# Quarter 0 scaled as rows before it is turned, and a fixed TensorE order around the first and the last products of the first feed-forward

## The chip, the core and the metric

The kernel runs on one core of a Trainium2 chip. Its engines work side by side, each through its own list of instructions in order: TensorE (PE, matrix products; its weight loads are listed as PEld), VectorE (DVE), ScalarE (ACT), GpSimd (POOL) and SyncE (SP, which here only issues DMAs). An instruction waits for what it reads and for the buffer that it writes; the order in each engine's list is made when the kernel is built. The metric is the device time of one execution in microseconds.

## The reference

One step of an encoder layer: a half-step SwiGLU feed-forward, a mixer of two branches (stick-breaking attention and a gated linear recurrence), a second half-step feed-forward, and a last norm. 1024 prompt frames with 16 meta tokens ahead, and 32 frames of a running stream, go through the same weights: T = 1072 tokens of 1024 channels. What the change touches is the first feed-forward and what it hands on:

```
def rmsnorm(x, g):
    y = xf * lax.rsqrt(jnp.mean(xf * xf, axis=-1, keepdims=True) + EPS)
    return (y * g.astype(jnp.float32)).astype(x.dtype)

def half_ffn(x, g, w_gate, w_up, w_down):
    h = rmsnorm(x, g)
    return x + 0.5 * ((jax.nn.silu(h @ w_gate) * (h @ w_up)) @ w_down)

    xp = concatenate([meta_tokens, x_prompt])        # 16 + 1024 rows
    x = half_ffn(x, ffn1_norm, ffn1_w_gate, ffn1_w_up, ffn1_w_down)
    h = rmsnorm(x, mix_norm)
    qa, ka, va, zf, ih, qh, g, ga, gb = split(h @ w_in)
    f = lb + (1.0 - lb) * sigmoid(zf)
```

## The kernel before

**Numbers.** Each factor of a product is split into a high and a low part (`split` L200, `weights` L167), and a product is three matmuls: high by high, high by low, low by high. `weights` loads a 128 by 1024 block of weights to a tile `raw` (two buffers), ACT copies it to `whi` (L184), DVE subtracts for `wlo` (L185); both have three buffers.

**Tiles.** In the first feed-forward the tokens stand in four quarters of QW = 268, and the 1024 channels in two halves (`kh`) of four 128-blocks. A quarter q is pair b = q // 2, side th = q % 2. `B[kh, th, b]` are the split, normalised activations of one half of one quarter (128 channels, four blocks, 268 tokens). Elsewhere tokens go in three tiles TT of 400, 384 and 288.

**Opening (L374 to L516).** Tokens come as rows: two tiles of 128 tokens for each quarter (`rows`), and `odds`, one tile that holds the last 12 tokens of each quarter at partitions 0, 32, 64, 96. POOL clears `odds` first. All these loads are issued on SP's queue, then the weights. `scales` (L392) makes the norm's factor of each token from rows: ACT squares with a running sum, two DVE steps, a power on POOL, four DVE steps. `spread` (L411) brings the factors of a quarter to all partitions: POOL multiplies the identity by the factors (`diag`, in the home of `ys`, shown as `t_ys`), PE multiplies ones by it, ACT copies the result to `R`. `columns` (L436) turns a quarter: for each of eight channel blocks three PE transposes into one PSUM bank, ACT copies the raw values to `x0` (stored to `x0_dram` for the residual), DVE multiplies by gain and R, and each half is then split into `B`. `first_units(0, columns_ahead)` (L487, L505) makes the first 128 gate and up columns: quarter by quarter 24 gate and 24 up matmuls, and ahead of quarter q the spread and the columns of quarter q + 1 (of 0 and 1 for the first). The order on PE is the planner's: it takes what it believes ready, by the program's order. `first_units(1, ...)` follows, `sums` (L456) makes the combinations of quarters for the later units, which take seven block products for eight (L531).

**End of the first feed-forward (L595 to L640).** `mid_dram` holds the 22 middle blocks. Eleven pairs of down weights are multiplied by them and added to `acc` (L633), for three token tiles and eight channel blocks. In the last pair, `after1` (L606) follows each token tile: it stores `acc`, calls `finish_one`, and `normalise` (L212): ACT makes `xh` (L216) and the squares (L222, L225), DVE makes `xl` (L217) and three of the squares' sums, POOL the other sums (L226). The two sum tiles `tot` have two buffers (`raw2`, shown as `t_raw`). The closure put into `waiting` (L234) is the rest: PE adds over partitions with ones, and `scale_rows` (L242) makes R on ACT (Ln, Exp) and POOL. `finish_one` runs all that wait.

**The first w_in products (L648 to L673).** `project_all` with the units of `zf` 0, 1 and 2 goes over token tiles, then units: 24 matmuls, DVE times R (L669), ACT sigmoid. After each token tile `between` calls `finish_one`.

**Order by hand.** `InOrder` (L88) chains PE's instructions in program order while `on` is true; in the parts above it is off. A `NoSync` dependency (`order`) only ties two instructions' places in the plan. `functions` (L109) loads a set of ACT functions.

Of the kernel before, what the change touches and what calls it, by code (L numbers as in the profile page):

```python
# [79 lines left out]
def tile_encoder_step(ctx, tc, x_prompt, x_sample, cache_k, cache_v, state_hgrn, meta_tokens,  # L80
# [70 lines left out]
    functions("natural_log_exp_and_others")  # L151

# [14 lines left out]
    def weights(parts, own=None):  # L167
        raw = wp.tile([P, D], F32, tag="raw", name="raw", bufs=2)
        n = 0
        for src, k in parts:  # L170
# [13 lines left out]
        A.activation(hi, raw, AF.Copy)  # L184
# [21 lines left out]
    homes = {"junk": ("ms", 1), "diag": ("ys", 1)}  # L206
# [55 lines left out]
    def ffn(pool, tiles, acc, xh, xl, R, w_gate, w_up, w_down, own, final, after, opening, later=None):  # L262
# [35 lines left out]
        def down(cs, mids, last):  # L298
            ws = [weights([(w_down[0][c * P:(c + 1) * P, :], 1)], own) for c in cs]
# [59 lines left out]
    with tc.tile_pool(name="f1", bufs=2) as pool:  # L359
# [8 lines left out]
        def load(dst, p0, t0, n):  # L368
            for src, c, r in sources:
                a, b = max(t0, c), min(t0 + n, c + r)  # L370
                if a < b:
                    nc.sync.dma_start(dst[p0 + a - t0:p0 + b - t0], src[a - c:b - c])
# [4 lines left out]
        rows = []  # L377
        for q in range(4):
# [5 lines left out]
            if q == 0:  # L384
                for x in range(4):
                    load(odds, 32 * x, x * QW + 2 * P, ODD)
# [5 lines left out]
        def scales(tiles):  # L392
# [3 lines left out]
            for j, xt in enumerate(tiles):  # L396
                for h in range(2):
                    junk = temp(pool, "junk")
                    A.activation(junk.bitcast(BF16)[:, :512], xt[:, h * 512:(h + 1) * 512], AF.Square,
                                 accum_out=ss[:, h, j:j + 1])  # L400
# [10 lines left out]
        def spread(q, r1, odd):  # L411
            diag = temp(pool, "diag")
            ps = bank(rotate=True)
            for h in range(2):
                c = slice(h * P, (h + 1) * P)
                G.tensor_scalar(diag[:, c], ident, r1[h], None, op0=ALU.mult)
                PE.matmul(ps[:, c], ones, diag[:, c], start=True, stop=True)
            p, c = slice(32 * q, 32 * q + ODD), slice(2 * P, QW)
            G.tensor_scalar(diag[p, c], ident[p, p], odd[p], None, op0=ALU.mult)
            PE.matmul(ps[:, c], ones[p], diag[p, c], start=True, stop=True)  # L420
            A.activation(R[:, q * QW:(q + 1) * QW], ps[:, :QW], AF.Copy)
# [14 lines left out]
        def columns(q):  # L436
            b, th = divmod(q, 2)
            for kh in range(2):
                x0 = f32s("s")
                v = value(kh, th, b)  # L440
                for k in range(4):
                    ps = bank(rotate=True)
                    ks = slice((4 * kh + k) * P, (4 * kh + k + 1) * P)
                    for h in range(2):
                        PE.transpose(ps[:, h * P:(h + 1) * P], rows[2 * q + h][:, ks], ident)
                    p = slice(32 * q, 32 * q + ODD)
                    PE.transpose(ps[:, 2 * P:QW], odds[p, ks], ident[p, p])
                    A.activation(x0[:, k], ps[:, :QW], AF.Copy)
                    V.scalar_tensor_tensor(v[:, k], ps[:, :QW], gains[:, 0, 4 * kh + k:4 * kh + k + 1],
                                           R[:, q * QW:(q + 1) * QW], op0=ALU.mult, op1=ALU.mult)  # L450
                nc.sync.dma_start(x0_dram[:, 4 * kh:4 * kh + 4, q * QW:(q + 1) * QW], x0)
                split(*B[kh, th, b], v)
# [34 lines left out]
        def first_units(c, before):  # L487
            gw = weights([(ffn1_w_gate[0][:, c * P:(c + 1) * P], KC)])
            uw = weights([(ffn1_w_up[0][:, c * P:(c + 1) * P], KC)])
            g = pool.tile([P, T], F32, tag="g", name="g", bufs=4)  # L490
            for q in range(4):
                before(q)
                b, th = divmod(q, 2)
                pss = []
                for wh, wl in (gw, uw):
# [9 lines left out]
        def columns_ahead(q):  # L505
            if q == 0:
                r = scales(rows[0:2] + [odds])
                found.append(r[2])
                spread(0, r[:2], found[0])
                columns(0)  # L510
# [964 lines left out]
```

## Time and profile before

| | us |
|---|---|
| median of three runs (2545.7 to 2548.61) | 2548.09 |
| the profiled execution | 2547.18 |
| its span, first to last instruction | 2545.4 |
| mean granted TensorE clock | 0.997 |
| PE busy in the first 73 us | 51.94 |
| DVE busy from 774 to 784 us, PE busy there | 10.00, 6.29 |

The span is divided among engines by busy time; times in the views are microseconds from the span's start, durations in us or (means) in ns. A line such as "PE a L100 <- POOL b L416: 5.7, 1, 5.7" says that PE's instruction at line 100, which writes a, waited 5.7 us in all for POOL's line 416, once, at longest 5.7. The chain of waits is followed back from the last instruction; its pieces have start, length, and what ran. In a timeline line the bracket is the engine's idle time before the instruction and what ended it. A window of the windows view lists length, then busy time and count for PE, PEld, DVE, ACT and POOL, then the granted clock, the DMA share and GB/s.

### The profile page before, as it was taken

To read this page: it belongs to the slowest core of one execution; us is meant where nothing else is said; L and a number is where in the kernel's file an instruction comes from. 1 tells how busy PE (TensorE), PEld (TensorE's weight loads), DVE (VectorE), ACT (ScalarE), POOL (GpSimd) and SP (SyncE) were. 2 spreads that over 40 slices of the span, in tenths; PEclk is the share of its full clock that TensorE was granted. 3 is DMA by queue.
4 is the path that set the end of the run, shared out by engine and by line. 5 is a ranking of instruction groups with operands and counts; after the bars stand their busy time and mean duration, and the time that the engine had idled before them with its cause. 6 is when DMAs were issued, how large, how long until landed. Compare 5 with 4: busy or idle time off the path is not lost.

```text
span 2545.4 us, 44180 instructions
## 1 busy us (share of the span) xinstructions
PE 2497.2 (98%) x18396; PEld 2397.6 (94%) x18396; DVE 1418.6 (56%) x2635; ACT 815.5 (32%) x1652; POOL 247.0 (10%) x388
## 2 busy tenths in 40 slices
PE   6999999999999999999999999999999999999998
PEld 5999999999998999998888888999999999999998
DVE  4655555577675467764655665557443444444445
ACT  6433333411124233332544543325211111111113
POOL 1000000000003012221000000214111001000100
PEclk9999999999999999999999999999999999999999
DMA  7122222352222111112111214321111111111112
GB/s 200 58 88 68 85 68 90 109 185 84 87 73 90 42 43 55 47 58 59 43 47 43 68 52 150 119 84 42 51 50 38 46 50 50 37 48 50 49 35 77
DMA packets 219182, 179.38 MB, mean 70 GB/s; under 512 B 37270, under 2 KB 202390, under 8 KB 218982
## 3 DMA queue, kind: packets, MB, share of 16 engines
q1 hardware_dynamic: 218950, 176.56, 22.3%
q8 instruction: 144, 2.36, 0.4%
q14 instruction: 56, 0.46, 0.1%
q0 software_dynamic: 32, 0.00, 0.0%
HBM read 137.78 MB, written 38.75 MB: 69 GB/s over the span
## 4 chain that ended last, share of the span: by engine, by line
PE 92%; DVE 5%; ACT 2%; issue 1%; DMA 1%; POOL 0%; SPq 0%; DVEq 0%; ACTq 0%; POOLq 0%
PE ps_z L100 37%; PE ps_mm L100 33%; PE ps_o L100 11%; PE ps_tr L100 8%; PE ps_tr L103 2%; DVE xl L217 1%; PE ps_z L103 1%; DVE wlo L185 1%; ACT whi L184 0%; PE ps_mm L103 0%; DVE left L993 0%; DVE acc L1381 0%; DMA xt<-in_x_prompt_dram 0%; DMA ga<-gate_dram 0%; DVE sd L875 0%
## 5 line engine op out<-in xcount | busy, mean ns | idle before, releaser
L100 PE MATMUL ps_mm<-xh,whi 128*128 128x384 f32 (+2 forms) x1224 | 405.4, 331 | 0.5 <-DVE raw L1201 0.5
L100 PE MATMUL ps_mm<-xh,wlo 128*128 128x384 f32 (+2 forms) x1224 | 399.1, 326 | 0.0
L100 PE MATMUL ps_mm<-xl,whi 128*128 128x384 f32 (+2 forms) x1224 | 398.2, 325 | 0.0
L184 ACT ACTIVATE whi<-raw 128x1024 fp32r<-128x1024 f32 x152 | 158.1, 1056 | 669.5 <-PE ps_z L100 429.4
L100 PEld LDWEIGHTS ps_mm<-xh,whi 128*128 128x128 f32 x1224 | 230.5, 188 | 9.1 <-issue 5.0
L100 PE MATMUL ps_z<-xh,whi 128*128 128x384 f32 (+2 forms) x720 | 234.9, 326 | 4.0 <-ACT whi L184 2.4
L100 PE MATMUL ps_z<-xh,wlo 128*128 128x384 f32 (+2 forms) x720 | 234.0, 325 | 0.1
L100 PE MATMUL ps_z<-xl,whi 128*128 128x384 f32 (+2 forms) x720 | 234.0, 325 | 0.0
L100 PEld LDWEIGHTS ps_mm<-xl,whi 128*128 128x128 f32 x1224 | 230.5, 188 | 1.2
L100 PEld LDWEIGHTS ps_mm<-xh,wlo 128*128 128x128 f32 x1224 | 230.7, 189 | 0.4
L185 DVE TENSOR_TENSOR wlo<-raw,whi 128x1024 fp32r<-128x1024 f32 x152 | 185.8, 1236 | 46.6 <-ACT whi L184 44.1
L100 PEld LDWEIGHTS ps_z<-xh,whi 128*128 128x128 f32 x720 | 136.1, 189 | 5.0 <-ACT whi L184 2.7
L286 POOL TENSOR_TENSOR g<-g,R 128x384 f32<-128x384 f32 (+1 forms) x66 | 77.7, 1178 | 641.4 <-ACT g L116 641.4
L993 DVE TENSOR_TENSOR_SCAN left<-left,oneb 128x512 f32<-128x512 f32 (+6 forms) x112 | 107.3, 958 | 54.8 <-ACT left L116 54.2
L100 PEld LDWEIGHTS ps_z<-xh,wlo 128*128 128x128 f32 x720 | 136.5, 190 | 0.9 <-DVE wlo L185 0.9
L100 PEld LDWEIGHTS ps_z<-xl,whi 128*128 128x128 f32 x720 | 136.2, 189 | 0.2
L287 DVE TENSOR_TENSOR g<-ps_z,g 128x384 f32<-128x384 f32 (+1 forms) x66 | 34.6, 524 | 179.1 <-PE ps_z L100 177.9
L116 ACT ACTIVATE g<-g 128x268 f32<-128x268 f32 (+2 forms) x126 | 58.1, 461 | 192.5 <-DVE g L284 148.3
L100 PE MATMUL ps_z<-ml,whi 128*128 128x384 f32 (+1 forms) x360 | 116.4, 323 | 0.0
L100 PE MATMUL ps_z<-mh,wlo 128*128 128x384 f32 (+1 forms) x360 | 115.8, 322 | 0.0
L100 PE MATMUL ps_z<-mh,whi 128*128 128x384 f32 (+1 forms) x360 | 115.7, 321 | 0.0
L100 PE MATMUL ps_z<-xe,whi 128*128 128x268 f32 (+3 forms) x424 | 111.9, 310 | 0.0
(581 smaller groups left out, 6240.7 us busy)
## 6 DMA issues: line engine op xcount, KB each, us to landing
raw<-in_ffn_w_gate_dram SPq DMA_DIRECT2D x44, 512.0 KB, 3.7
raw<-in_ffn_w_up_dram SPq DMA_DIRECT2D x44, 512.0 KB, 3.6
raw<-in_ffn_w_down_dram SPq DMA_DIRECT2D x44, 512.0 KB, 4.3
raw<-in_w_in_dram SPq DMA_DIRECT2D x44, 512.0 KB, 3.8
mid_dram<-g SPq DMA_DIRECT2D x22, 536.0 KB, 2.7
mid<-mid_dram SPq DMA_DIRECT2D x22, 536.0 KB, 3.7
gate_dram<-gst SPq DMA_DIRECT2D x32, 192.0 KB, 1.9
acc<-x_dram SPq DMA_DIRECT2D x3, 1536.0 KB, 6.7
```

The lines of the kernel that those rows point to most:

```text
L100: return self.queue(nc.tensor.matmul(*args, **more))
L103: return self.queue(nc.tensor.transpose(*args, **more))
L116: i = A.activation(out, in_, func, **more).ins
L184: A.activation(hi, raw, AF.Copy)
L185: V.tensor_tensor(lo, raw, hi.bitcast(F32), op=ALU.subtract)
L217: V.scalar_tensor_tensor(xl[:, k, s], srcs[k], g, xh[:, k, s].bitcast(F32), op0=ALU.mult, op1=ALU.subtract)
L286: G.tensor_tensor(g[:, :n], g[:, :n], R[:, s], op=ALU.mult)
L287: V.tensor_tensor(g[:, :n], pu[:, :n], g[:, :n], op=ALU.mult)
L993: V.tensor_tensor_scan(rev(st[:rows]), rev(st[:rows]), one, 1.0 if carry is None else carry[:rows], op0=ALU.mult, op1=ALU.mult)
```

## The change

It has these parts.

1. The odd rows are loaded on ACT's queue; the first gate and up weights are issued on SP's queue right after quarter 0's rows, ahead of the rows of quarters 1 to 3.
2. Quarter 0: `raw_columns` transposes it unscaled and DVE copies it to `x0`. Then its rows are scaled in place by the norm's factors (ACT one tile, DVE the other and the odd rows), transposed again (`scaled_columns`), and split straight from PSUM: ACT makes high and plain values, DVE the low part. Spread 0 goes.
3. DVE makes the diagonals in place of POOL, in a tile of their own; the Squares of quarters 1 to 3 are tied on ACT behind a given instruction (`behind`).
4. In unit 0, spread and columns of quarter q + 1 stand between the half products of quarter q, and PE's order is fixed from the raw transposes to unit 0's last product. Unit 1's weights are tied behind a late ACT instruction.
5. In the last down pair PE's order is fixed until the zf products are through. The first zf weights are asked for before that pair. The sums over partitions go singly: tile 0's after six blocks of tile 2, the others each after a zf product. The sigmoids wait for the last sum.
6. A first load of an ACT function set goes; two small DVE steps (`lmax`, `causalb`) are tied behind the latest product.

```diff
-    functions("natural_log_exp_and_others")
-    homes = {"junk": ("ms", 1), "diag": ("ys", 1)}
+    homes = {"junk": ("ms", 1)}
...
-    def weights(parts, own=None):
+    def weights(parts, raw=None, own=None, behind=None):
...
+        made = A.activation(hi, raw, AF.Copy).ins
+        if behind is not None:
+            tc.add_manual_dep(made, behind.name, order, reason="order")
...
-                    load(odds, 32 * x, x * QW + 2 * P, ODD)
+                    load(odds, 32 * x, x * QW + 2 * P, ODD, nc.scalar)
+                for raw, w in zip(first, (ffn1_w_gate, ffn1_w_up)):
+                    nc.sync.dma_start(raw.rearrange("p (k m) -> p k m", k=KC),
+                                      w[0][:, :P].rearrange("(k p) m -> p k m", p=P))
...
+        latest = [None]
+        def scales(tiles, behind=None):
...
+                    latest[0] = A.activation(junk.bitcast(BF16)[:, :512], xt[:, h * 512:(h + 1) * 512],
+                                              AF.Square, accum_out=ss[:, h, j:j + 1]).ins
+                    if behind is not None:
+                        tc.add_manual_dep(latest[0], behind.name, order, reason="order")
...
+        def diagonals(q, r1, odd):
+            diag = pool.tile([P, QW], F32, tag="diag", name="diag", bufs=3)
+            for h in range(2):
+                c = slice(h * P, (h + 1) * P)
+                V.tensor_scalar(diag[:, c], ident, r1[h], None, op0=ALU.mult)
...
+        def raw_columns():
+            for kh in range(2):
+                x0 = f32s("s")
+                for k in range(4):
+                    V.tensor_copy(x0[:, k], turned(0, 4 * kh + k))
+                nc.sync.dma_start(x0_dram[:, 4 * kh:4 * kh + 4, :QW], x0)
+
+        def scale_rows_of(r):
+            for kh in range(2):
+                ks = slice(kh * 512, (kh + 1) * 512)
+                latest[0] = A.activation(rows[0][:, ks], rows[0][:, ks], AF.Copy, scale=r[0]).ins
+                V.tensor_scalar(rows[1][:, ks], rows[1][:, ks], r[1], None, op0=ALU.mult)
+                V.tensor_scalar(odds[:ODD, ks], odds[:ODD, ks], r[2][:ODD], None, op0=ALU.mult)
+
+        def scaled_columns():
+            for kh in range(2):
+                h, l = B[kh, 0, 0]
+                v = value(kh, 0, 0)
+                for k in range(4):
+                    g = gains[:, 0, 4 * kh + k:4 * kh + k + 1]
+                    ps = turned(0, 4 * kh + k)
+                    latest[0] = A.activation(h[:, k], ps, AF.Copy, scale=g).ins
+                    V.scalar_tensor_tensor(l[:, k], ps, g, h[:, k].bitcast(F32), op0=ALU.mult, op1=ALU.subtract)
+                    A.activation(v[:, k], ps, AF.Copy, scale=g)
...
                     for kh in range(2):
                         ks = slice(kh * 512, (kh + 1) * 512)
                         product(ps, (wh[:, ks], wl[:, ks]), B[kh, th, b], kh == 0)
+                        between(q, 2 * j + kh)
...
+        def next_columns(q, step):
             if q < 3:
+                if step == 0:
+                    spread(q + 1, diags.pop(0))
+                    if q < 2:
+                        diags.append(scaled_diagonals(q + 2))
+                elif step < 3:
+                    columns(q + 1, step - 1)
+
+        def scaled_diagonals(q):
+            return diagonals(q, scales(rows[2 * q:2 * q + 2], latest[0]), odd_scale)
+
+        PE.on = True
+        raw_columns()
+        r = scales([rows[0], odds, rows[1]])
+        ws = [weights([], first[0], behind=latest[0])]
+        odd_scale = r[1]
+        scale_rows_of([r[0], r[2], r[1]])
+        ws.append(weights([], first[1], behind=latest[0]))
+        scaled_columns()
+        diags = [scaled_diagonals(1)]
+        first_units(0, next_columns, ws)
+        PE.on, PE.last, third = False, None, latest[0]
...
-            finish_one()
             normalise(pool, chunks(acc, t0, n), xh1, xl1, 1, R1, t0, n)
...
             if final:
                 functions("natural_log_exp_and_others")
+                zf_first = weights([(w_in[0][:, COL_ZF:COL_ZF + P], KC)])
+                PE.on = True
...
                 for m in range(KC):
                     one(m, t0, n)
+                    if final and j == 2 and m == 5:
+                        waiting.pop(0)()
...
-                if between:
-                    between()
+                    if between:
+                        between()
...
+                raw_gates.append(z)
+                if not waiting:
+                    if table["name"] != "sigmoid_and_others":
+                        functions("sigmoid_and_others")
+                    while raw_gates:
+                        z = raw_gates.pop(0)
+                        act(z, z, AF.Sigmoid)
...
-        project_all([zf_unit(h) for h in range(3)], TT, True, finish_one)
+        project_all([zf_unit(h) for h in range(3)], TT, True, lambda: waiting and waiting.pop(0)(), [zf_first])
+        PE.on, PE.last = False, None
```

More of the change, by code (lines that the diff above doesn't have):

```diff
@@ L165, in tile_encoder_step @@
     big = Wide
-    def weights(parts, own=None):
-        raw = wp.tile([P, D], F32, tag="raw", name="raw", bufs=2)
-        n = 0
-        for src, k in parts:
+    def weights(parts, raw=None, own=None, behind=None):
+        n, loaded = 0, raw is not None
+        if not loaded:
+            raw = wp.tile([P, D], F32, tag="raw", name="raw", bufs=2)
+        for src, k in () if loaded else parts:
             m = src.shape[-1]
@@ L377, in tile_encoder_step @@
         rows = []
+        first = [wp.tile([P, D], F32, tag="raw", name="raw", bufs=2) for _ in range(2)]
         for q in range(4):
@@ L434, in value, with turned @@
             return last[b] if (kh, th) == (1, 0) else plain[b][:, {(0, 0): 0, (0, 1): 1, (1, 1): 2}[kh, th]]
-        def columns(q):
-            b, th = divmod(q, 2)
+        def turned(q, k):
+            ps = bank(rotate=True)
+            ks = slice(k * P, (k + 1) * P)
+            for h in range(2):
+                PE.transpose(ps[:, h * P:(h + 1) * P], rows[2 * q + h][:, ks], ident)
+            p = slice(32 * q, 32 * q + ODD)
+            PE.transpose(ps[:, 2 * P:QW], odds[p, ks], ident[p, p])
+            return ps[:, :QW]
@@ L503, in first_units @@
             nc.sync.dma_start(mid_dram[c], g)
[L505 to L510, printed above, removed]
-            if q < 3:
-                spread(q + 1, scales(rows[2 * q + 2:2 * q + 4]), found[0])
-                columns(q + 1)
-        found = []
-        first_units(0, columns_ahead)
+        def next_columns(q, step):
+            if q < 3:
+                if step == 0:
[17 more added lines that the diff above has]
+        PE.on, PE.last, third = False, None, latest[0]
         t4s = [sums(b) for b in range(2)]
-        first_units(1, lambda q: None)
+        first_units(1, lambda q, step: None, [weights([(w[0][:, P:2 * P], KC)], behind=third)
+                                              for w in (ffn1_w_gate, ffn1_w_up)])
         constants()
@@ L646, in project, with project_all @@
             project_all([(col, evac)], tiles)
-        def project_all(units, tiles=TT, rotate=False, between=None):
-            ws = [weights([(w_in[0][:, col:col + P], KC)]) for col, _ in units]
+        def project_all(units, tiles=TT, rotate=False, between=None, ws=None):
+            ws = ws or []
+            ws = ws + [weights([(w_in[0][:, col:col + P], KC)]) for col, _ in units[len(ws):]]
             pending = []
```

57 lines of the change are left out of this document (24 added, 33 removed).

## The prediction

> **What bounds the kernel now.** First the busy times of the page: TensorE (PE) is busy 98% of the span, so time can be won only where PE stands still or runs slowly.
>
> ```profile
> PE 2497.2 (98%) x18396; PEld 2397.6 (94%) x18396; DVE 1418.6 (56%) x2635; ACT 815.5 (32%) x1652; POOL 247.0 (10%) x388
> ```
>
> That leaves 2545.4 - 2497.2 = 48.2 us of idle PE. Second, the waits of PE, in the stretches that the diff touches: 0 to 75 us, then 745 to 835 us (total, times, longest).
>
> ```profile
> PE ps_z L103 <- DMA xt<-in_x_prompt_dram: 8.6, 2, 7.0
> PE ps_mm L100 <- POOL t_ys L416: 5.7, 1, 5.7
> PE ps_z L100 <- POOL t_ys L416: 3.8, 1, 3.8
> PE ps_mm L100 <- DVE acc0s L449: 2.8, 1, 2.8
> ```
>
> ```profile
> PE ps_z L100 <- ACT whi L184: 2.4, 1, 2.4
> PE ps_z L100 <- POOL t_raw L226: 1.8, 1, 1.8
> PE ps_z L100 <- DVE t_raw L226: 1.4, 1, 1.4
> ```
>
> Some 21 us of waits stand before the first product and 5.6 around the last products of the first feed-forward. Third, the chain of waits in order of time (start, us) gives the marks to measure against.
>
> ```profile
> 18.06 1.92 PE ps_mm L100 x6
> 19.98 0.84 PE ps_mm L103 x3
> ...
> 37.02 4.97 PE ps_mm L100 x24
> 41.99 2.96 PE ps_z L100 x24
> 44.95 0.76 PE ps_tr L100 x6
> 45.71 0.53 PE ps_z L103 x3
> ...
> 787.58 6.21 PE ps_z L100 x22
> 793.79 8.58 PE ps_mm L100 x48
> ```
>
> Read: 24 products take 4.97 us at first and 2.96 later; a spread (six matmuls of ones by a diagonal) 1.92, later 0.76; a group of three transposes 0.84, later 0.53. **Mark one** is 44.95: quarter 0's gate and up products done, quarter 1's spread and columns done too. **Mark two** is 793.79: the first two zf units have done their first token tile and all three sums of squares are through PE. Fourth, the timeline, for the pace of PE.
>
> ```profile
> 40.54 0.43 PE L100 MATMUL ps_mm<-xh0s,whi 128*128 128x268 f32 x1
> 40.76 0.37 PE L100 MATMUL ps_mm<-xl0s,whi 128*128 128x268 f32 x1
> ```
>
> At 40.5 us PE still runs at half pace: products start 0.22 us apart, later 2.96/24 = 0.12. The spread at 18.06 and the eight groups of transposes behind it, some 7 us, did not end that; 3.8 us of unbroken products from 37.02 did (the matmul at 40.76 is the first shorter one).
>
> **The opening, part by part.** Removed: spread 0, its copy to R and the splits of quarter 0. Added: a second pass of transposes, because quarter 0 is now turned raw (for x0), scaled in place, and turned again; all of it, and everything up to unit 0's last product, in one fixed PE order.
>
> ```profile
> 6.96 0.63 ACT L399 ACTIVATE t_ms<-xt 128x512 bf16<-128x512 f32 x1 [3.65 <-DMA xt<-in_x_prompt_dram]
> 10.09 0.69 PE L103 MATMUL ps_z<-cst,xt 128*128 128x128 f32 x2 [1.58 <-DMA xt<-in_x_prompt_dram]
> 11.56 0.39 PE L103 MATMUL ps_z<-cst,odds 12*128 12x12 f32 x2
> 15.08 0.16 DVE L402 TENSOR_TENSOR ss<-ss 128x3 f32<-128x3 f32 x1 [11.66 <-ACT t_ms L399]
> 17.13 0.16 DVE L408 TENSOR_TENSOR ss<-ss 128x3 f32<-128x3 f32 x1
> 28.23 0.63 ACT L399 ACTIVATE t_ms<-xt 128x512 bf16<-128x512 f32 x1
> 28.77 0.19 ACT L399 ACTIVATION_READ_ACCUMULATOR t_ms<-xt 128x1 f32 x1
> L448 ACT ACTIVATE s<-ps_z 128x268 f32<-128x268 f32 x16 | 6.4, 405 | 1.3 <-PE ps_z L103 0.6
> L947 DVE TENSOR_SCALAR xs<-xs 128x384 f32<-128x384 f32 x8 | 2.8, 354 | 4.7 <-POOL xs L946 4.7
> ```
>
> 1. Each group now needs both row tiles and the odd rows at once. The second row tile is there at 10.09, the odd rows by 11.56 (their landing isn't shown). Their four DMAs go to ACT's queue behind POOL's memset; ACT has nothing before 6.96. The first two weights move ahead of the later rows on SP's queue; they and the odd rows may hold up the second row tile. I take 10.5; bounds 9.7 and 12.5.
> 2. Eight raw groups at 0.83 (0.84 in the chain): to 17.1. DVE copies them out, under PE's pace.
> 3. Six Squares of about 0.75 (0.63 and the accumulator's read) on ACT end near 13; the scale chain takes 17.3 - 15.1 = 2.2, with DVE copies in between about 3; DVE may run a weight split (1.2) ahead of it. Then the rows are scaled, 0.63 a half on ACT, about 0.4 a half twice on DVE (nearest row: 354 ns for 384 columns). The second pass starts near 17.9: 0.8 lost (bounds 0 and 3).
> 4. Eight scaled groups: to 24.5. ACT makes two copies a group, 0.41 each, just under PE's pace. So the first product starts at 24.5, not 37.02.
> 5. Twelve products of 0.22 (gate, first half): to 27.2. Then the fixed order demands spread 1. Its Squares are tied on ACT behind quarter 0's last scaled copy (24.9; the last plain copy 25.2): four of 0.75 to 28.2, chain 2.2 to 30.4, first diagonal on DVE and its hand-over 0.4 (bounds 0.16, the three-column step, and 0.7, two of the 354 ns) to 30.8. **PE waits 3.6 us where before it had work to reorder.** Queued behind that wait are all later products; nobody else needs them yet.
> 6. Spread 1, 1.9: to 32.7. Twelve products, of which the last few at full pace, 2.3: to 35.0. Then columns 4 x 0.53, products 1.5, columns 2.1, products 1.5: to **42.2, against mark one at 44.95: 2.75 us won.** Of the 12.5 us that the first product comes earlier, quarter 1's work, formerly ahead of it, takes back the most.
>
> After that each quarter is 4 x 1.5 + 0.76 + 4.2 = 10.9 us of PE, and a half's columns are wanted some 3.7 us or more after their last transpose, while evacuation and split (about 0.5, 1.1 on ACT, 1.3 on DVE) take 3. Cost nothing by that cover; if DVE's scale steps come between, under 1 us per quarter (kept in the range). The x0 stores, the dropped table load (ACT idle until 6.96) and the later lmax and causalb are off the path.
>
> **The end of the first feed-forward.**
>
> ```profile
> 749.15 2.36 DVE L185 TENSOR_TENSOR wlo<-raw,whi 128x1024 fp32r<-128x1024 f32 x2
> ...
> 773.21 0.29 PE L100 MATMUL ps_tr<-S,wlo 128*128 128x288 f32 x1
> 775.35 1.56 PE L100 MATMUL ps_z<-t_raw,cst 128*128 128x384 f32 x4 [1.85 <-POOL t_raw L226]
> 776.45 0.64 PE L100 MATMUL ps_o<-xh,whi 128*128 128x400 f32 x1
> ...
> 776.19 7.55 DVE L217 SCALAR_TENSOR_TENSOR xl<-acc,gains,xh 128x288 fp32r<-128x288 f32 x8
> 783.66 2.43 DVE L226 TENSOR_TENSOR t_raw<-t_raw,t_g 128x288 f32<-128x288 f32 x2
> 786.01 3.46 DVE L185 TENSOR_TENSOR wlo<-raw,whi 128x1024 fp32r<-128x1024 f32 x2
> 791.41 0.54 PE L100 MATMUL ps_z<-xl,whi 128*128 128x400 f32 x1
> 784.00:788.00 4.00, 2.48 (x7) 1.21 (x6) 3.90 (x4) 0.53 (x1) 3.75 (x4) 0.63 0.00 0
> ```
>
> The down products end at 773.5, a sum takes 1.1 (775.35 to 776.45), a zf unit's tile 4.3 (half of 8.58). Two units and two sums are 10.8 us; mark two comes 20.3 after 773.5, so 9.5 are lost. Unit 1's low weights come only after DVE's eight xl and two adds, which follow each other without a gap from 776.19 to 786, and that sets 787.58. The granted clock is 0.63 there (the number after the busy times) and matmuls still take 0.54 at 791.4. In the new order unit 0 follows the last down product at about 773.5 without waiting for a sum (the 1.8 goes), then comes sum 1, then unit 1. Sum 2's tiles have two buffers, freed by sum 1 on PE, which now runs 4 us later: so its Squares, and DVE's two adds (2.43), fall behind unit 1's weights. These end about 2.4 us earlier: third matmul at 785.2, unit 1 done 6.2 later at 791.4 (the clock falls again in this longer wait), and sum 2, now behind it, about 1.1: 792.5 against mark two, 793.8. **Won 1.3.** At the start of the final pair, PE can no longer take the next outputs' first halves while the second weight is split: its low part is done at 749.15 + 1.2 = 750.4, in-order PE wants it at 749.5: up to 0.9 lost, mostly hidden behind DVE, which sets 787.58 anyway; I take 0.3 (bounds 0 and 0.9).
>
> **Sum:** 2.75 + 1.3 - 0.3 = 3.75 us. The profiled execution lasted 2547.18 us (span 2545.4): 2543.4. The median shown, 2548.09, is 0.9 above it: **2544.3 us**. A measurement here tells about 0.2%, 5.1 us, from no change; so the forecast is a gain below that.
>
> **Rivals.**
> *Half pace lasts (slower).* In step 6 spread 1 and its products are 4.6 us of real matmul work, then transposes follow; the rows show 3.8 us needed from 37.02, and from 787.58 a matmul at 791.41 that still takes 0.54. If 4.6 doesn't do, columns, products and columns run at 0.83 and 0.22, and full pace returns only in the long run of products after them, near 49.8. By then PE has G1's first 12 products done, where before it had spread 2 and 8 groups done: 3.6 us lost instead of 2.75 won, 6.4 us more: **2550.7**; with the opening 2.5 us late as well, 2553.2 and beyond. [...]
> *Low weights ahead (faster).* If unit 1's split comes before some xl on DVE, unit 1 follows sum 1 at once, at full clock, and most of the 9.5 us lost there comes back, some 7 beyond the 1.3 counted: **about 2537**. For it: unit 1's buffer is free from 773.5, long before xl ends. Against: xl stands earlier in the program, and is ready.
> *The opening pays in full.* If the scales of quarter 1 are early enough that PE never stops between 24.5 and 29, full pace comes at 28.3 and mark one at 37.8: **2540.0**. Against: the tie on ACT.
> *It doesn't do what it says:* the second pass waits as long as spread 0 did; then the opening wins nothing, 2547. It lies within the forecast's own range, 2541 to 2548.
>
> **How the numbers follow.** Forecast 0.47; half pace 0.28; low weights ahead 0.17; full opening 0.08. Faster by over 0.2% (below 2543.0): 0.17 + 0.08 + 0.05 of the forecast's = 0.30. Slower (above 2553.2): 0.12 of the half-pace case's 0.28. Within: 0.58. The range, 2536 to 2554, takes in half pace with a late opening, and low weights ahead.
>
> **What would show it.** Raw transposes from 10.5 and scaled from 17.9, first product at 24.5; one PE wait of 3.6 us on diag ahead of spread 1; the pace of the products after it (0.22 or 0.12) decides the first rival. At the end: no wait on t_raw at 773; wlo of unit 1 on DVE before or after xl decides the second. Wrong if the odd rows land after 12.5, or PE starves in quarters 1 to 3.

## The result, and the profile after

The changed kernel took 2553.95 us (median of 20 runs, 2547.68 to 2555.86), the kernel before 2548.02 on the same chips: the ratio, taken over all runs and not from the two medians, is 1.0019, with a 95% interval of 1.0012 to 1.0026. It is slower by 0.2%, where the forecast was a gain of 3.75 us. Of all runs of this document three took 4406 to 7445 us; they are left out of the ratios and of the ranges given below. The profiled execution lasted 2555.25 us. Its page begins with PE's busy time:

```profile
PE 2510.1 (98%) x18414; PEld 2407.0 (94%) x18414; DVE 1422.9 (56%) x2654; ACT 817.3 (32%) x1658; POOL 238.8 (9%) x376
```

PE is busy 12.9 us longer than before, with 18 matmul records more (24 transposes more, six matmuls of spread 0 less), and idle 4.8 us less (2553.5 - 2510.1 = 43.4 against 48.2). So waits did go away; what came in their place is PE running slower. The waits of PE in the same two stretches as before (0 to 75 us, then 745 to 835 us) say which went:

```profile
PE ps_mm L103 <- DMA xt<-in_x_prompt_dram: 8.7, 2, 5.7
PE ps_z L100 <- DVE diag L424: 4.5, 1, 4.5
PE ps_mm L103 <- ACT xt L484: 3.5, 1, 3.5
PE ps_mm L103 <- DMA odds<-in_x_prompt_dram: 1.3, 1, 1.3
PE ps_o L100 <- DVE xl1s L203: 0.6, 1, 0.6
PE ps_z L100 <- DVE xl1s L203: 0.6, 1, 0.6
...
```

```profile
PE ps_o L100 <- DVE wlo L186: 3.1, 1, 3.1
PE ps_z L100 <- DVE wlo L186: 0.6, 1, 0.6
PE ps_o L100 <- ACT whi L183: 0.5, 1, 0.5
```

In the opening, the two waits on POOL's diagonals (5.7 and 3.8) and the one on DVE's first scaled columns (2.8) have become a wait on the scaled rows (3.5) and one on DVE's diagonal (4.5). At the end of the feed-forward the waits for sums (t_raw, 1.8 and 1.4) are gone and 4.2 remain.

Where the time went is read best by counting. Every kernel here issues 14,400 products in the same stages, so the start of the n-th product can be compared between traces. Worked out from the traces, in us (the first column of times is the kernel before; the others are differences from it; product 384 is the first behind the two `first_units`, 5000 lies among the down products, 5500 behind mark two, 8000 in the attention, 8600 among the branch products that follow it; the lower six rows are explained below). The expectations and the text from here on call what starts at product 384 "unit 1": it is the first call of `unit` (i = 1), while the second `first_units` is products 192 to 383.

```
product              0     384    5000    5500    8000    8600   14399
before           37.02   96.58  719.38  814.37 1416.31 1588.41 2533.15
after            -9.52   +4.45   +4.24   +1.50   +3.02   +8.23   +8.08
opening_alone   -10.71   +2.49   +1.99   +1.11   +2.78   +4.18   +4.00
end_alone        -1.01   -0.87   -0.87   -3.26   -1.57   -0.64   +0.32
banks_back      -10.38   +3.15   +2.65   +1.30   +1.51   +1.84   +1.84
banks_moved      -1.91   -0.93   -0.94   -1.92   -0.32   +0.79   +0.60
squares_early   -10.54   -2.21   -2.43   -5.00   -3.26   -2.19   -1.48
squares_again   -10.62   -2.62   -2.77   -5.44   -5.23   -4.45   -3.13
```

The row "after" has four parts. The first product comes 9.5 us earlier; unit 1, all the same, starts 4.45 later; the end of the feed-forward wins 2.7 back (4.24 to 1.50); and 6.6 us are lost by the end where the diff changes nothing: 1.5 before product 8000, 5.2 between 8000 and 8600, less 0.15 that comes back. (The profiled run of before was itself a little late: the four others with its opening reach product 384 between 0.85 and 1.03 us earlier.)

The late loss shows in the granted clock (the column behind POOL's). The window view of the changed kernel at the end of the attention:

```profile
1560.00:1565.00 5.00, 5.00 (x50) 4.72 (x48) 4.56 (x11) 4.23 (x12) 0.18 (x1) 1.00 0.01 4
1565.00:1570.00 5.00, 5.00 (x38) 4.40 (x36) 2.69 (x9) 1.85 (x3) 0.00 (x0) 0.64 0.08 30
1570.00:1575.00 5.00, 5.00 (x30) 4.08 (x29) 1.34 (x5) 0.91 (x3) 0.00 (x0) 0.50 0.81 267
1575.00:1580.00 5.00, 5.00 (x31) 4.31 (x30) 1.12 (x4) 0.44 (x1) 0.00 (x0) 0.50 0.15 51
1580.00:1585.00 5.00, 5.00 (x21) 5.00 (x20) 5.00 (x12) 0.00 (x0) 0.00 (x0) 0.65 0.47 147
```

PE is busy in every one of these microseconds, and the clock is halved for 17.07 us, five times 3.413, from 1566.45 on. In the profile of before, none of this stretch ran at a lower clock. The times and lengths of half clocks in this document are read from the clock records in the traces of these runs. In that of after, the ten changes of the clock between 30.45 and 2549.49 us lie 1, 2, 219, 1, 120, 1, 106, 5 and 283 times 3.413 us apart; in that of before, the four between 40.94 and 2539.49 lie 218, 2 and 512 times as far. A window, here and in the expectations, is one such 3.413 us. The timeline says what PE was busy with when the clock fell:

```profile
1563.30 0.30 PE L100 MATMUL ps_o<-aT,vs 32*64 32x32 f32 x2
1563.43 0.86 PE L100 MATMUL ps_o<-aT,vc 16*64 16x32 f32 x10
1564.22 0.30 PE L100 MATMUL ps_o<-aT,vs 32*64 32x32 f32 x2
1564.36 0.86 PE L100 MATMUL ps_o<-aT,vc 16*64 16x32 f32 x10
1565.15 0.44 PE L100 MATMUL ps_mm<-xh,whi 128*128 128x384 f32 x1
1565.52 0.30 PE L100 MATMUL ps_o<-aT,vs 32*64 32x32 f32 x2
1565.65 0.86 PE L100 MATMUL ps_o<-aT,vc 16*64 16x32 f32 x10
```

These are the attention's last pieces: matmuls of 16 or 32 rows and 32 columns, with one wide product (128 rows, 384 columns) in 3.2 us. In the kernel before, five wide products stood in a row among the same pieces:

```profile
1560.41 0.30 PE L100 MATMUL ps_o<-aT,vs 32*64 32x32 f32 x2
1560.55 0.86 PE L100 MATMUL ps_o<-aT,vc 16*64 16x32 f32 x10
1561.34 0.30 PE L100 MATMUL ps_o<-aT,vs 32*64 32x32 f32 x2
1561.48 0.86 PE L100 MATMUL ps_o<-aT,vc 16*64 16x32 f32 x10
1562.26 0.45 PE L100 MATMUL ps_mm<-xh,whi 128*128 128x384 f32 x1
1562.55 0.34 PE L100 MATMUL ps_mm<-xl,whi 128*128 128x384 f32 x1
1562.72 0.34 PE L100 MATMUL ps_mm<-xh,wlo 128*128 128x384 f32 x1
1562.90 0.51 PE L100 MATMUL ps_mm<-xh,whi 128*128 128x384 f32 x2
1563.34 0.30 PE L100 MATMUL ps_o<-aT,vs 32*64 32x32 f32 x2
```

The order of PE there has changed, and no line of the diff touches that place. What does is a counter. `bank(rotate=True)` gives out eight PSUM banks in turn. The old opening drew 36 times (4 spreads, 32 groups of transposes), the new one 43 (3 spreads, 40 groups). So from the opening on, each user of the rotation has a bank seven places further on, and the scheduler, which is free at the branch products, puts them in another order. That is the theory; the runs below test it. In all 16 profiled runs PE's order there is one of two: that of before wherever the branch products have the old banks (nine profiled runs), that of after wherever they have the new ones (seven).

### The profile page after: what moved, and what is told of

The parts are those of the page before. It is cut to its first block, busy times and chain, and to the rows that moved or that the text cites. A ratio compares the mean times of both kernels' runs of the same rounds, so it can differ in the third digit from the quotient of the medians.

```text
span 2553.5 us, 44227 instructions
## 1 busy us (share of the span) xinstructions
PE 2510.1 (98%) x18414; PEld 2407.0 (94%) x18414; DVE 1422.9 (56%) x2654; ACT 817.3 (32%) x1658; POOL 238.8 (9%) x376
## 4 chain that ended last, share of the span: by engine, by line
PE 92%; DVE 4%; ACT 2%; issue 1%; POOL 1%; DMA 0%; DVEq 0%; ACTq 0%; POOLq 0%
PE ps_z L100 36%; PE ps_mm L100 33%; PE ps_o L100 11%; PE ps_tr L100 8%; PE ps_tr L103 2%; PE ps_z L103 1%; DVE xl L218 1%; PE ps_mm L103 1%; DVE wlo L186 1%; ACT whi L183 0%; DVE acc L1452 0%; DVE left L1064 0%; DVE acc L691 0%; DMA odds<-in_x_prompt_dram 0%; DVE sd L946 0%
## 5 line engine op out<-in xcount | busy, mean ns | idle before, releaser
L100 PE MATMUL ps_z<-xh,whi 128*128 128x288 f32 (+2 forms) x704 | 228.7, 325 | 0.0
L100 PE MATMUL ps_z<-xh,wlo 128*128 128x288 f32 (+2 forms) x704 | 228.6, 325 | 0.0
L100 PE MATMUL ps_z<-xl,whi 128*128 128x288 f32 (+2 forms) x704 | 228.4, 324 | 0.0
L203 DVE TENSOR_TENSOR wlo<-raw,whi 128x1024 fp32r<-128x1024 f32 (+1 forms) x40 | 38.3, 959 | 105.5 <-ACT whi L202 104.3
L100 PE MATMUL ps_z<-xe,whi 128*128 128x268 f32 (+3 forms) x424 | 96.4, 310 | 0.0
```

Of the source, the lines that this page charges most:

```text
L100: return self.queue(nc.tensor.matmul(*args, **more))
L203: V.tensor_tensor(dst_l, src, dst_h.bitcast(F32), op=ALU.subtract)
```

## The experiments

Each time was measured against the kernel before on the same chip; the runs of one job share these. In brackets stand the median of the kernel before, the ratio and its 95% interval. An expectation is quoted under each edit.

**after_again**: the changed kernel, no edit.

> The changed kernel once more, unchanged. In 13 of its 20 runs it took 2553.5 to 2555.9 us, in the profiled one with a half clock of five windows at 1566. Theory (the order of the branch products, which gives one window or five by where the free-running windows fall): the slow group shows again, in 4 or more of 11 runs, median 2550 to 2555. Rival (chance, or the chip that it ran on): no run above 2552.5, median 2549 to 2551.5, as for the same kernel with the old banks.

2550.19 us (11 runs; before 2547.14; ratio 1.0015, 1.0006 to 1.0024). The runs fall in groups: five at 2547.9 to 2548.1, two at 2550.2 and 2550.7, four at 2555.5 to 2555.7. The upper group shows again, but in 4 of 11 instead of 13 of 20. The profiled run was one of the lower group and had no half clock in the attention. The mean granted clock of each run tells the groups apart: 0.993 or 0.994 in the upper four, 0.997 or 0.998 in the other seven; and of the first 20 runs, 0.993 or 0.994 in the upper 13, 0.995 or more in the other seven. So the size of the result depends on how many runs fall in the upper group, and 1.0019 is one draw of it.

**banks_back** and **banks_moved**: the same counter turned, once in each direction.

```diff
# banks_back, on the changed kernel
+        rot[0] += 1
         mids = {}
         for m in range(KC):
             mids[m] = merge(m)
# banks_moved, on the kernel before
+        rot[0] += 7
         mids = {}
```

> The changed kernel, with one more draw from the rotation of PSUM banks ahead of the second feed-forward's branch products, so that these fall on the banks that they had before. Theory (the order): the changed opening draws 43 rotating banks where it drew 36; so the first branch products stand elsewhere between the thin products of the attention's last pieces, PE's clock halves there for 17.07 us (1566.7 in the profile of after) and some 6.6 us are lost. With the old banks no half clock near 1560 to 1590, and the median falls from 2553.95 to 2547 to 2549. Rival (the phase): only the place of the clock's 3.41 us windows relative to the kernel decides; then the halving stays, in about two runs of three, and the median stays at 2553 to 2555.

2550.42 us (before 2547.73; 1.0010, 1.0001 to 1.0019), all 11 runs between 2548.3 and 2551.7: the upper group is gone, and so is the half clock:

```profile
1560.00:1565.00 5.00, 5.00 (x48) 4.42 (x46) 4.31 (x9) 3.80 (x9) 0.00 (x0) 1.00 0.08 30
1565.00:1570.00 5.00, 5.00 (x58) 4.27 (x56) 2.07 (x6) 1.37 (x3) 0.00 (x0) 1.00 0.09 17
```

The same thin pieces run here at a clock of 1.00, and the table has +1.51 at product 8000 and +1.84 at 8600. The median came 1.4 us above what the theory gave. The theory had taken off all 6.6 us of the late loss, though 1.5 of them stand before product 8000, ahead of the place where the counter is turned; the rest stays open.

> The kernel before, with seven more draws from the rotation of PSUM banks ahead of the second feed-forward's branch products, and nothing else. Theory (the order): the branch products stand as in the changed kernel, the clock halves near 1560 in most runs, and the median rises from 2548.0 to 2552 to 2555. Rival (the phase): no change, 2547 to 2549.

2548.66 us (before 2547.73; 1.0006, 0.9997 to 1.0014): neither theory's number. The runs lay in two groups, six at 2544.2 to 2548.7 and five at 2550.9 to 2552.3; the profiled one had a half clock of a single window at 1563.55. That left open whether the order does it alone.

**opening_alone** (the changed kernel with the end of the feed-forward as before) and **end_alone** (the kernel before with the new end): the two halves of the change. The edits are the hunks of the diff from `after1` to `zf_unit`, taken back or applied.

> The changed kernel with its old end of the first feed-forward: the new opening alone, with the bank rotation that comes with it. Theory: the opening loses 4.5 us by the start of unit 1 (101.19 against 96.74), the late half clock costs some 6 more in most runs, and the 2.8 us that the new end wins are missing: median 2556 to 2558, unit 1's start some 4.5 us later than before, mark two some 4.5 later than before. Rival (the opening itself wins as forecast and what was seen is chance): unit 1's start at 94 to 95.

2549.99 us (before 2547.73; 1.0010, 1.0002 to 1.0019), far below the 2556 expected, with no run above 2551.2. The opening's loss is there (+2.49 us at unit 1 and +4.00 at the end in its profile, with a half clock of one window at 1566.84; +2.3 in the medians), and the upper group is missing although PE's order at the branch products is that of the changed kernel.

> The kernel before with the new end of the first feed-forward alone (first zf weight ahead, fixed order, sums one by one). Theory: the new end wins 2.5 to 3 us between pair 9 and mark two, nothing else moves: median 2545 to 2546, mark two at 790.5 to 791.5 against 793.79. Rival (the end won only what the opening's delay had put under cover, or the forecast's 1.0): median 2547 or above, mark two at 792.5 or later.

2545.02 us (before 2547.73; 0.9990, 0.9982 to 0.9999). As expected: 2.7 us faster, and unit 1 not moved.

**squares_new_banks** (squares_early, below, without the turned counter), **opening_again** and **banks_moved_again** (no new edit) go at the open point: is the order enough?

> squares_early, but with the bank rotation left as the changed opening makes it, so that PE's order from the end of the first feed-forward on is that of the changed kernel. Theory (order of the branch products, with the windows' place deciding between one half window and five): a slow group some 5 us above the fast one in some of the runs (of the changed kernel's 31 runs 17 stood above 2553), and the fast group at 2543 to 2546 as for squares_early; in the profile a half clock that begins between 1555 and 1565, which squares_early did not have. Rival (the slow group belongs to the changed opening's own lateness, not to the order): all runs within 2543 to 2547, no half clock there.

2548.52 us (before 2548.23; 1.0000, 0.9991 to 1.0008), where squares_again took 2544.71 in the same job: eight of 11 runs at 2547.8 to 2549.3, three at 2542.3 to 2545.7. Half clock for five windows from 1559.85. The theory's case.

> opening_alone once more. Theory (the order makes a long half clock possible, the place of the windows decides): a slow group, some 4 to 5 us above the others, in 3 or more of 11 runs, that is at 2553 to 2557. Rival (something besides the order is needed, which the old end of the first feed-forward takes away): all runs within 2548 to 2552 again.

2551.10 us (before 2548.33; 1.0017, 1.0008 to 1.0026): five of 12 runs at 2555.2 to 2557.7, the other seven at 2548.2 to 2551.1; half clock for five windows from 1566.57 in the profiled run.

> banks_moved once more: the kernel before with the branch products on other banks. Theory (the order): two groups again, one at 2544 to 2549 as for the kernel before, one at 2550.5 to 2552.5 where the kernel before has had no run out of 119, with 3 or more of 11 runs in it. Rival: all runs within 2544.5 to 2549.5.

2550.83 us (before 2548.33; 1.0010, 1.0002 to 1.0019): ten of 11 runs at 2550.0 to 2551.8, where the kernel before had none above 2549.1 in that job; half clock for five windows from 1562.35. With nothing but seven draws more from a counter, the kernel before becomes 2.5 us slower here (0.9, within noise, in the first job).

So the order makes the long half clock possible, and something that differs from run to run decides. The traces show what: the half stretches begin and end on that grid of 3.413 us, and its place relative to the kernel's start differed from run to run (the times divided by 3.4133 us leave 3.39 us in before, 3.14 in after, and 3.26, 2.46, 3.37, 0.24 and 0.12 for the other five beginnings in the table). Seven profiled runs have the new order, and six of them had a half clock there. Take its beginning and move it back by that run's delay at product 8000 (all in us):

```
                    begins   delay   moved back   lasts
opening_again      1566.57   +3.57      1563.00   17.07
banks_moved_again  1562.35   -0.99      1563.34   17.07
after              1566.45   +3.02      1563.43   17.07
squares_new_banks  1559.85   -3.64      1563.49   17.07
banks_moved        1563.55   -0.32      1563.87    3.41
opening_alone      1566.84   +2.78      1564.06    3.41
```

The thin stretch of the new order is 4.1 us long at full clock (1561.80 to 1565.87 in after_again, the seventh run). In the four runs with a long half clock, 2.7 to 3.2 us of it lay in the window at whose end the clock fell, and 0.9 to 1.4 were left for the next window. In the two with a single half window the whole window lay in it, and 0.4 to 0.6 were left. In after_again a boundary at 1563.95 cut it into 2.2 and 1.9 us, and the clock held. So the clock fell behind each window that held 2.7 us of thin pieces or more and held behind the two with 2.2 and 1.9, and with a boundary 0.4 us later (1563.49 against 1563.87 on the moved scale) there was a single half window in place of five. These numbers are read from seven runs. Why the clock then stays low for five windows is open, and so is why more runs fall in the upper group than a place by chance on the grid would give.

The old order isn't free of half clocks: end_alone, squares_early, squares_again and free_order have a single half window that begins between 1583.4 and 1586.5, behind a wait of PE of some 2 us for DVE's `ga`. None of the nine has one in the thin pieces.

**squares_early**, **free_order**, **values_later**, **columns_together** take the opening apart. All stand on banks_back.

```diff
# squares_early
         r = scales([rows[0], odds, rows[1]])
+        r_next = scales(rows[2:4])
         ws = [weights([], first[0], behind=latest[0])]
...
-        diags = [scaled_diagonals(1)]
+        diags = [diagonals(1, r_next, odd_scale)]
# free_order
-        PE.on = True
         raw_columns()
# values_later
                     V.scalar_tensor_tensor(l[:, k], ps, g, h[:, k].bitcast(F32), op0=ALU.mult, op1=ALU.subtract)
-                    A.activation(v[:, k], ps, AF.Copy, scale=g)
+                G.tensor_tensor(v, h.bitcast(F32), l.bitcast(F32), op=ALU.add)
# columns_together, on squares_early
-                elif step < 3:
-                    columns(q + 1, step - 1)
+                elif step == 1:
+                    for kh in range(2):
+                        columns(q + 1, kh)
```

> banks_back with quarter 1's four Squares and scale chain issued right behind quarter 0's own, without the tie behind quarter 0's scaled copies. Theory (the tie, and ACT's plain copies that end only at 29.9, make the wait on diag): diagonals are ready before 28, the wait of 4.5 us goes, and unit 1 starts 3.5 to 4.5 us earlier than in banks_back, median 2546 to 2548. Rival: the Squares push the scaling of quarter 0's rows and the first weights back, the second pass starts 1.5 us later, and the win is under 2 us: median 2549 to 2550.

2545.49 us (before 2547.14; 0.9987, 0.9978 to 0.9997). The wait on the diagonal is gone; spread 1 starts at 29.33 instead of 35.04 in the changed kernel, unit 1 at 94.36 instead of 99.72 in banks_back. That is 5.4 us for a wait of 4.5. Spread 1 in banks_back, then in squares_early:

```profile
34.19 1.72 PE L100 MATMUL ps_z<-diag,cst 128*128 128x128 f32 x6 [4.50 <-DVE diag L424]
```

```profile
29.33 1.58 PE L100 MATMUL ps_z<-diag,cst 128*128 128x128 f32 x6
```

> The changed kernel with the old banks for the branch products (as banks_back) and without the fixed PE order in the opening: the scheduler may put quarter 0's other 36 products ahead of spread 1. Theory (PE's 4.5 us wait for the diagonal is paid because the order forbids those products): the wait on diag falls under 1 us, unit 1 starts 3 to 4.5 us earlier than in banks_back, median 2546 to 2548. Rival (the wait moves: quarter 1's products then wait for its columns): another PE wait of 3 us or more before quarter 1, unit 1 no earlier, median 2549.5 to 2551.

2546.97 us (before 2547.14; 0.9996, 0.9987 to 1.0005). Unit 1 starts at 95.90, 3.8 earlier than in banks_back. Not all of that is the diagonal's wait: the first product is already 1.9 earlier (24.73 against 26.64), since the free order also moves the transposes. The diagonal's 4.5 us fall to 0.4; waits of 1.6 and 0.6 on quarter 1's first half are new, 2.2 together where the rival gave one of 3 or more:

```profile
PE ps_z L100 <- ACT xh2s L202: 1.6, 1, 1.6
...
PE ps_z L100 <- DVE xl2s L203: 0.6, 1, 0.6
...
PE ps_z L100 <- DVE diag L424: 0.4, 1, 0.4
```

> banks_back with quarter 0's plain scaled copies (eight of 0.37 us on ACT) taken off ACT: the values are made by POOL from the high and the low part instead. Theory (ACT at two copies a group is slower than PE, so that Squares begin at 29.3): Squares begin at 26 to 27, the wait on diag falls from 4.5 to 1 to 2 us, unit 1 starts 2.5 to 3.5 us earlier than in banks_back, median 2547 to 2548.5. Rival (Squares were held by the tie's last copy alone, at 28.5): the wait falls by under 1.5 us.

2549.31 us (before 2547.14; 1.0007, 0.9998 to 1.0016). The rival's number: the wait on the diagonal fell only from 4.5 to 3.2. ACT's timeline has the first Square at 27.21, straight behind the last high copy (26.83), where it was 29.26 in the changed kernel; that copy is what the tie names. So the tie costs more than the plain copies.

```profile
26.83 0.48 ACT L496 ACTIVATE xh0s<-ps_z,gains 128x268 fp32r<-128x268 f32 x1 [0.34 <-PE ps_z L103]
27.21 0.62 ACT L406 ACTIVATE t_ms<-xt 128x512 bf16<-128x512 f32 x1
```

> squares_early with both halves of the next quarter's columns behind the second twelve products of a quarter instead of one half behind the second and one behind the third. Theory (quarters 1 to 3 lost 2 us to two waits of 0.6 for the last low part and to 0.37 us a quarter at the switches between transposes and products): from the 48th to the 192nd product 28 to 28.6 us instead of 29.84, median 0.8 to 1.5 below squares_early. Rival (less cover for the second half's split): a wait on xl1s of over 0.6 in each quarter, no gain.

2545.28 us (before 2548.23; 0.9992, 0.9983 to 1.0001), against 2544.71 of squares_again in the same job. From the end of the 48th product to the end of unit 0 it took 28.83 us instead of 29.84 in squares_early, less of a gain than expected; a wait of 1.8 on ACT's Silu is new, and in the profiled run a half clock of two windows from 37.8 puts unit 1 at 96.81, 2.5 later than in squares_early. In the median, no gain:

```profile
PE ps_mm L100 <- ACT g L116: 1.8, 1, 1.8
```

**end_again** and **squares_again**: the two that were below the kernel before, side by side.

> end_alone once more, to stand beside squares_early's line on the same chip. Theory (new end wins 2.5 to 3 by itself): ratio to the kernel before 0.9985 to 0.9995, median 2.2 to 3.2 us below it. Rival (chance in the first look): within 1 us of the kernel before.

> squares_early once more, on the chip that runs end_again. Theory (the opening then wins about 1 us beside the new end's 2.7): 0.5 to 1.5 us below end_again, 3 to 4 us below the kernel before. Rival (the opening's win is given back in the clock windows behind it): within 0.5 us of end_again.

Before 2548.23; end_again 2546.37 (0.9994, 0.9985 to 1.0003); squares_again 2544.71 (0.9986, 0.9978 to 0.9995). squares_early, the changed kernel with its Squares moved ahead and its banks turned back, is faster than the kernel before in each of its two jobs (by 1.65 and 3.5 us), and than after_again (2550.19) in the job that they share. The new end alone was measurably faster in one job of two: end_again's 1.9 us is less than expected, and its interval takes in no change.

## Why the prediction was wrong

Two parts of the sum failed. The opening, forecast to win 2.75 us, lost 4.45 by unit 1. And the sum has no term for the stages behind mark two, where 6.6 us were lost, 5.2 of them in the branch products. The gap of 7.2 us in the opening, forecast against the profile of after, has four pieces: the first product is 3.0 late (steps 3 and 4), the wait of step 5 with the spread behind it is 1.0 longer, the pace of step 6 costs 1.1, and quarters 1 to 3, put at nothing, cost 2.1. That 2553.95 lies inside the stated range, by 0.05, is luck: the range reached that far for half pace with a late opening.

By its own steps, each against the profile of after. The rows are DVE's, ACT's and PE's timeline of the opening:

```profile
17.31 0.15 DVE L411 TENSOR_TENSOR ss<-ss 128x3 f32<-128x3 f32 x1
...
19.34 0.16 DVE L417 TENSOR_TENSOR ss<-ss 128x3 f32<-128x3 f32 x1
...
19.42 1.22 DVE L186 TENSOR_TENSOR wlo<-raw,whi 128x1024 fp32r<-128x1024 f32 x1
...
20.37 0.48 PE L103 MATMUL ps_mm<-cst,xt 128*128 128x128 f32 x1 [3.45 <-ACT xt L484]
...
27.50 0.59 PE L100 MATMUL ps_mm<-xh0s,whi 128*128 128x268 f32 x1
...
28.53 0.53 ACT L496 ACTIVATE xh0s<-ps_z,gains 128x268 fp32r<-128x268 f32 x1
...
29.26 0.69 ACT L406 ACTIVATE t_ms<-xt 128x512 bf16<-128x512 f32 x1
...
34.60 0.48 DVE L424 TENSOR_SCALAR diag<-cst,ss 128x128 f32<-128x128 f32 x2
...
35.04 1.72 PE L100 MATMUL ps_z<-diag,cst 128*128 128x128 f32 x6 [4.49 <-DVE diag L424]
...
39.31 0.43 PE L100 MATMUL ps_mm<-xh0s,wlo 128*128 128x268 f32 x1
...
42.06 0.39 PE L100 MATMUL ps_o<-xh0s,whi 128*128 128x268 f32 x1
```

1. *Raw transposes at 10.5*: right for quarter 0 (the first group has its odd rows at 10.88). But ACT's Squares take all the odd rows, and the last of these, the stream's, held ACT for 4.7 us until 12.72, just past the 12.5 that the prediction names as a sign. Step 2, eight groups at 0.83: right.
2. *Second pass from 17.9 (step 3)*: it starts at 20.37. The Squares, put at 13, end at 15.71. The scale chain begins only at 17.31, behind the last raw copy in DVE's queue, and takes 2.2; then the scaling. In banks_back the Squares end at 14.86, and the chain again stands behind the last copy. The prediction had let it run among the copies. The weight split that it named does come ahead. Of the 2.5 us, 0.4 is the start.
3. *First product at 24.5 (step 4)*: 27.50, 3.0 late, by step 3 and 0.5 more (the first group waits once for the second row tile's scaling). The profiled run was a late one: in the four others with this opening unchanged it comes at 26.31 to 26.88.
4. *Diagonal at 30.8, a wait of 3.6 (step 5)*: the wait was foreseen, but not its price, and that decides the opening's sign. The Squares, put at 25.2 on the sum that ACT makes its two copies of a group as PE turns it, begin at 29.26. ACT's queue takes the high copies first, each idle 0.34 for PE's next group, and eight plain ones from 25.51 on between and behind them; the last high copy, which the tie names, comes at 28.53. The diagonals come at 34.60 and the wait is 4.5. squares_early shows the price: with the Squares ahead and untied 5.4 us come back at unit 1 (the sum had 3.6), and the opening then wins there, 1.3 to 1.7 against the four others with the old opening.
5. *The last products behind the spread at full pace (step 6)*: no. All twelve ran at 0.22 (36.69 to 39.31), full pace came at 40.7. The trace's clock record shows the course: the clock did rise at 30.45, behind products that ran from 27.50, and it fell again at 33.86, behind a window in which PE stood waiting. The window view has the stretch:

```profile
30.00:34.00 4.00, 0.55 (x3) 0.23 (x2) 0.49 (x3) 2.47 (x8) 0.71 (x1) 0.98 0.50 4
34.00:40.00 6.00, 4.96 (x20) 4.50 (x20) 1.20 (x6) 3.10 (x9) 0.00 (x0) 0.50 0.02 5
```

   A whole window of full clock, 30.45 to 33.86, was granted to a PE that was busy for 0.10 of it (0.55 in the 4 us of the first line). So the half clock came back behind the wait, which the prediction's sum left out. This differed from run to run: with this wait (4.5, in values_later 3.2) the clock rose and fell in after, opening_again and values_later (unit 1 at +4.0 to +4.5), and came once, behind the spread, in after_again, opening_alone and banks_back (+2.5 to +3.2). In opening_again the clock rose at 30.58 behind 3.41 us of which PE was busy for 2.72, while it didn't rise behind 1.98 in after_again and 1.93 in opening_alone. In squares_early the clock rises at 31.2 and stays. Mark one, forecast at 42.2, lay at 47.29.
6. *Quarters 1 to 3 at no cost*: 2.0 us, from the end of the 48th product to the end of unit 0 (29.89 against 27.91), in two quarters: each has a wait of 0.6 on the low part, and some 0.4 more where PE changes between transposes and products more often. The prediction had kept "under 1 us per quarter" in the range, which just holds.
7. *The end of the feed-forward, 1.3 less 0.3*: better than forecast. From product 5000 to 5500 the eleven profiled runs with the new end won 2.27 us on average, the five with the old one 0.41 (against before), so 1.9 net. The split of zf unit 1's low weight does come ahead of the last adds, as forecast, though behind an evacuation that waited for POOL; the third matmul is at 788.77, a wait of 3.1:

```profile
786.92 0.57 DVE L732 TENSOR_TENSOR acc<-ps_tr,R 128x400 f32<-128x400 f32 x1 [0.92 <-POOL R L253]
787.41 3.04 DVE L186 TENSOR_TENSOR wlo<-raw,whi 128x1024 fp32r<-128x1024 f32 x2
790.38 2.03 DVE L227 TENSOR_TENSOR t_raw<-t_raw,t_g 128x288 f32<-128x288 f32 x2
```

   What was mis-sized is the clock: runs with one half window there (3.41 us from 788.21 in after) won 2.4 to 2.7, those with two 1.35 to 1.7.
8. *Nothing moves behind mark two*: the prediction didn't even say it. It had no term for the late stages, and 6.6 of the 8.1 us of the profiled run were lost there. Without the upper group of runs the change would have cost some 1 to 3 us (the lower five runs of after_again +0.9, banks_back +2.7); with it, the median is 5.9 us slower.

Of the rivals, "half pace lasts" has the right sign, and its number (2550.7) lies among the lower runs, but not the right course: full pace came back at 40.7, before the columns were through. No run shows the 0.28 that it was given: of the six profiled runs with the long wait for the diagonal, the clock rose before it and fell again in three, and rose only behind the spread in three. "Low weights ahead" didn't happen: xl stands ahead of wlo on DVE. "The opening pays in full" needed the early scales, and the tie forbade them, as the prediction said against it. "It doesn't do what it says" is out: the first product came 9.5 us earlier.

The late loss is shown to come from the bank rotation (banks_back, banks_moved_again, squares_new_banks). A further 1.5 us between products 7000 and 8000, with a single half window at 1201 in the profile of after, can't be laid to the change: it also came and went among kernels that are alike there (+1.5 in end_alone, none in end_again).

## What to carry to other kernels

A change can act through a counter that it never names: look for what is shared in turn (banks, buffers, queues) and ask whether the number of draws has changed, and compare the order of instructions in the stages that the diff doesn't touch. A wait of PE cost more here than its length (5.4 us came back in squares_early for one of 4.5), and in after half clock stood behind it from 33.86 to 40.69; so in an order fixed by hand, what the first waiting instruction needs (here the diagonal) must be made early, by engines that stand idle (here ACT from 16.7 to 19.6), not behind work that is wanted later. And where the clock changes at other places from run to run, as here, one kernel has several times: a profile shows one of them, and a change of 0.2% needs many runs. The mean granted clock of each run sorts them (0.993 or 0.994 in the upper runs of the changed kernel, 0.995 or more in the others).

## What the hardware showed that was not expected

- The clock was halved while PE was busy without a gap (5.00 of each 5 us in the window view). The matmuls were small: 16 or 32 rows by 32 columns, with one wide product among them, and one started every 0.08 us. Five wide products in a row, 1.1 us of them, stood there in the nine profiled runs with the old order, and the clock held in each; with the single one it fell in six of seven. So the busy time of the view didn't tell here when the clock would fall. Whether it is the few rows and columns that count, or gaps between short matmuls that the view doesn't show, these runs don't tell apart. Every half stretch inside the kernels lasted 1, 2, 3 or 5 times 3.413 us in the clock records.
- Once lost in such a stretch, the clock stayed low for five windows (17.07 us) or for one (3.41), with a difference of 0.4 us in where the grid lay (squares_new_banks against banks_moved).
- In the opening, the view of the granted clock reads 1.00 before its first record (28 to 30 us) while products start 0.22 us apart: there the pace tells the clock, and not that column.
